# First layer's modulation vectors 2 to 5: dot products on VectorE in place of products on TensorE

## The chip, the cores and the metric

The kernel runs on one core of a Trainium2 chip. The metric is the device time of one launch in microseconds. Before the change it is 2318.97 us, the median of three runs (2317.82 to 2321.76).

## The reference

Two layers of a trunk over 640 tokens of width 1024: 128 context tokens and 512 latent tokens that share all weights. Each layer first computes its modulation from the conditioning vector (one for each of the two token groups), six vectors of 1024:

```
mod_ctx = silu(c_ctx) @ w_mod[l] + b_mod[l]      # w_mod[l]: 1024 x 6144
mod_lat = silu(c)     @ w_mod[l] + b_mod[l]
sh1, sc1, g1, sh2, sc2, g2 = split(mod, 6)       # vectors 0 to 5
h = rmsnorm(x, norm1_g) * (1 + sc1) + sh1
x = x + g1 * mixer(h)                            # attention, conv, pool, gMLP; gates; w_out
h = rmsnorm(x, norm2_g) * (1 + sc2) + sh2
x = x + g2 * (relu(h @ w_mlp_in) ** 2 @ w_mlp_out)
```

Vectors 0 and 1 are needed at the very start of a layer, vector 2 where the mixer's output projection is added, 3 and 4 at the second norm, 5 in the MLP. All is float32, and the large matrix products are made of three products of split operands (high by high, high by low, low by high).

## The kernel before

**Tiling.** Activations lie with 128 channels on the partitions and the 640 tokens along the free axis. Weights come as slabs of 128x1024 (512 KB). Each slab is loaded by SP into one of four buffers tagged `raw` (L251, L235), and split by ACT (`h`, L240) and VectorE (`l`, L241) into one of three pairs of buffers. TensorE multiplies from these at L362, in output tiles of 128x640 with 48 or 24 matmuls.

**Order of the work.** TensorE and SP run in the order in which the program is written out (`manual_schedule`). On VectorE, ACT and GpSimd a list scheduler decides: among instructions that are ready it takes the one that was written out first, and `later(-n)` moves an instruction n places ahead (slab splits by 2500, evacuations of PSUM by 1000). From gates(3) to the second gate of branch 1 VectorE too runs in written order (`byhand`, L1251 to L1284). A layer of the mixer goes: q, k, v and rotary (`qk`); attention, into which `_weave` (L1241) mixes the products of `fill()` (two convolution inputs, L948, and eight gates of branch 0, L1120); the gMLP's v (`sgu_v`, L1016); branch 0 and the gMLP outputs; gates and branches 3, 2; gates of branch 1 with the end of the convolution (`conv_out`); branch 1; the output projection (`project`, L554).

**Attention's chain.** For each head and each of four blocks of queries: scores in PSUM (L846), row maximum on VectorE (L848), exponential on ACT (L849), reciprocal and scaling on VectorE (L850, L851). For each of five blocks of keys (L857): transposes into the one PSUM buffer `pt`, a copy to `h` by ACT (L240), a subtraction to `l` by VectorE (L241), then two products with the values (L865). The buffer `pt` is free for the next key block when the subtraction is done.

**Modulation.** Vectors 0 and 1 of layer 0 come from `start()` (L1170) on TensorE. Vectors 2 to 5 of layer 0 come from `mod_steps` (L429): blocks of `w_mod` are loaded into two `md` buffers (L439), multiplied on TensorE by silu(c) as 32-column weights in four column groups (L447), copied by ACT (L450), transposed (L454), copied again (L456) and added up on VectorE (L460, L461). All of layer 1's vectors come from `mod_dots` (L464) during layer 0's MLP: rows of the transposed `w_mod` are loaded into `raw` buffers (one block is 128 outputs by 1024 inputs), and VectorE multiplies each with silu(c), once for each token group, and accumulates along the row (L490).

**Side work.** Both are generators in the list `side`; `tick()` (L500) runs the first one up to its next `yield`, and `flush()` runs all to the end. `mod_steps` is appended before gates(3) and is advanced by the ticks of gates and branches from there to the `flush()` before branch 1 (L1287).

Of the kernel before, what the change touches and what calls it, by code (L numbers as in the profile page):

```python
# [140 lines left out]
def trunk(ctx, tc, a, o):  # L141
# [287 lines left out]
    def mod_steps(l, g, mk):  # L429

        wv = a["w_mod"].rearrange("d (v h n) -> d v h n", v=6, h=2)
        bm = lcol[l][:, C_BMOD:C_BMOD + 48].rearrange("p (v c) -> p v c", v=6)
        for half in range(2):
            for kp in range(4):
                rr = []
                for i in range(2):
                    k = 2 * kp + i
                    t_ = mk().rearrange("p (v n) -> p v n", v=2)
                    sp.dma_start(out=t_, in_=wv[k * P:(k + 1) * P, 2 * g:2 * g + 2, half, :])  # L439
                    rr.append([t_[:, j] for j in range(2)])  # L440
                    yield
                if kp == 0:
                    t = psum("pt")
                for i in range(2):
                    for j in range(2):
                        q = 2 * i + j
                        pe.matmul(t[32 * q:32 * q + 32], sv3[:, 2 * kp + i, :], rr[i][j], start=kp == 0, stop=kp == 3)  # L447
            rows, cols = tmp(512), tmp(512)
            with later(-EVAC_FIRST):
                act.activation(rows, t, AF.Copy)  # L450
            yield
            tr = psum("pt")
            for nb in range(4):
                pe.transpose(tr[:, nb * P:(nb + 1) * P], rows[:, nb * P:(nb + 1) * P], ident)  # L454
            with later(-EVAC_FIRST):
                act.activation(cols, tr, AF.Copy)  # L456
            tv = cols.rearrange("p (n q m) -> p q n m", q=4, m=32)
            for j in range(2):
                dst = mod3(l, 2 * g + j)[:, 4 * half:4 * half + 4, :]
                vec.tensor_tensor(dst, tv[:, j, :, 0:2], tv[:, 2 + j, :, 0:2], ALU.add)  # L460
                vec.tensor_tensor(dst, dst, bm[:, 2 * g + j, 4 * half:4 * half + 4, None].to_broadcast([P, 4, 2]), ALU.add)  # L461
            yield True

    def mod_dots(l, mp):  # L464


        sw, junk = maker(mp, "sw", 1, 2 * D)(), maker(mp, "junk", 1, D)
        sp.dma_start(out=sw, in_=a["crow"])
        th_ = junk()
        s3 = [sw[:, s * D:(s + 1) * D] for s in range(2)]  # L470
        yield
        for z in s3:
            act.activation(th_, z, AF.Tanh, scale=0.5)
            vec.scalar_tensor_tensor(z, th_, 1.0, z, ALU.add, ALU.mult)
        bm = lcol[l][:, C_BMOD:C_BMOD + 48].rearrange("p (v c) -> p v c", v=6)
        blocks = [(v, c) for v in (1, 0, 2, 4, 3, 5) for c in range(KC)]

        def fetch(v, c):
            t = raw_tile()
            sp.dma_start(out=t, in_=a["w_modt"][v, c])  # L480
            return t

        w = fetch(*blocks[0])
        yield
        for i, (v, c) in enumerate(blocks):
            wn = fetch(*blocks[i + 1]) if i + 1 < len(blocks) else None
            dst = mod3(l, v)
            for s in range(2):
                out = w if s else junk()
                vec.scalar_tensor_tensor(out, w, 0.5, s3[s], ALU.mult, ALU.mult, accum_out=dst[:, c, s:s + 1])  # L490
            if c == KC - 1:
                vec.tensor_tensor(dst, dst, bm[:, v, :, None].to_broadcast([P, KC, 2]), ALU.add)
            w = wn
            yield
# [3 lines left out]
    taps = [iter(())]  # L498

    def tick(n=0):  # L500
        for _ in range(n):
            next(taps[0], None)
        while side:
# [631 lines left out]
    def branch(bi, gs, br, merged, mg):  # L1135
        for mp in range(4):
            w = use("b", bi, mp)
            for m in (2 * mp, 2 * mp + 1):
# [8 lines left out]
                tick(TAPS[1])  # L1147
# [61 lines left out]
    for l in range(DEPTH):  # L1209
# [3 lines left out]
        with opened(f"mx{l}") as mx:  # L1213
# [13 lines left out]
            with opened(f"at{l}") as ap:  # L1227
# [4 lines left out]

                def fill():
                    for c in range(2, 4):
                        ys.append((yield from conv_in(l, c, h, cv)))
# [251 lines left out]
```

## Time and profile before

| | |
|---|---|
| median of three runs | 2318.97 us |
| the profiled execution's own time | 2326.15 us |
| its span, first to last instruction | 2324.4 us |
| mean granted TensorE clock | 0.992 |
| TensorE busy | 2254.2 us (97%) |
| VectorE busy | 1655.0 us (71%) |
| ACT busy | 856.4 us (37%) |
| GpSimd busy | 70.4 us (3%) |
| stages, by the trace | attention of layer 0 about 118 to 272 us, gates(3) from 364, `flush()` before branch 1 at about 647, output projection from 676, layer 1 from 1192 |

A matmul's busy time overlaps the next one's, so pitches (from one start to the next) are used for TensorE. Idle time of an engine is the length of a stretch less its busy time there.

### The profile page before, as it was taken

To read this page: it belongs to the slowest core of one execution; us is meant where nothing else is said; L and a number is where in the kernel's file an instruction comes from. 1 tells how busy PE (TensorE), PEld (TensorE's weight loads), DVE (VectorE), ACT (ScalarE), POOL (GpSimd) and SP (SyncE) were. 2 spreads that over 40 slices of the span, in tenths; PEclk is the share of its full clock that TensorE was granted. 3 is DMA by queue.
4 is the path that set the end of the run, shared out by engine and by line. 5 is a ranking of instruction groups with operands and counts; after the bars stand their busy time and mean duration, and the time that the engine had idled before them with its cause. 6 is when DMAs were issued, how large, how long until landed. Compare 5 with 4: busy or idle time off the path is not lost.

```text
span 2324.4 us, 36290 instructions
## 1 busy us (share of the span) xinstructions
PE 2254.2 (97%) x15050; PEld 2182.7 (94%) x15050; DVE 1655.0 (71%) x2557; ACT 856.4 (37%) x1296; POOL 70.4 (3%) x188
## 2 busy tenths in 40 slices
PE   6999999999999999999999999999999999999997
PEld 5989899989999999999998898999999999999987
DVE  6676457678777776766477773687897788777776
ACT  5455342222335332222254553422224453232233
POOL 1100000000000000000011000000000000000001
PEclk9999999999999999999999999999999999999999
DMA  7421122333343444444354212222222432222223
GB/s 285 113 84 60 63 70 99 133 136 136 126 138 127 154 154 146 151 148 146 108 175 107 78 46 69 73 78 64 65 76 92 150 109 65 73 85 89 73 91 110
DMA packets 77253, 252.43 MB, mean 109 GB/s; under 512 B 11808, under 2 KB 12832, under 8 KB 76960
## 3 DMA queue, kind: packets, MB, share of 16 engines
q1 hardware_dynamic: 66592, 224.56, 29.9%
q0 software_dynamic: 9920, 24.89, 3.8%
q8 instruction: 118, 1.93, 0.3%
q10 hardware_dynamic: 576, 0.66, 0.1%
q14 instruction: 47, 0.39, 0.1%
HBM read 238.65 MB, written 10.75 MB: 107 GB/s over the span
## 4 chain that ended last, share of the span: by engine, by line
PE 66%; issue 24%; DVE 6%; ACT 2%; DMA 1%; POOL 0%; SPq 0%; DVEq 0%; ACTq 0%; POOLq 0%
PE ps L362 44%; PE ph L362 5%; PE pt L653 4%; DVE l L241 2%; PE sc L653 2%; PE pt L857 1%; PE sc L846 1%; PE po L865 1%; PE sc L362 1%; ACT h L240 1%; PE po L653 1%; PE sc L1031 1%; DMA st<-in_w_mod 1%; PE pt L447 1%; PE sc L414 1%
## 5 line engine op out<-in xcount | busy, mean ns | idle before, releaser
L362 PE MATMUL ps<-h,h 128*128 128x320 f32 x5296 | 1119.3, 310 | 12.8 <-ACT gx L1132 4.7
L362 PEld LDWEIGHTS ps<-h,h 128*128 128x128 f32 x5296 | 862.7, 188 | 31.9 <-ACT h L240 12.5
L362 PE MATMUL ps<-h,l 128*128 128x320 f32 x3408 | 835.7, 309 | 0.0
L240 ACT ACTIVATE h<-raw 128x1024 fp32r<-128x1024 f32 x337 | 357.2, 1060 | 976.7 <-PE ps L362 658.8
L362 PEld LDWEIGHTS ps<-h,l 128*128 128x128 f32 x3408 | 585.6, 188 | 0.0
L241 DVE TENSOR_TENSOR l<-raw,h 128x1024 fp32r<-128x1024 f32 x337 | 411.6, 1222 | 217.5 <-ACT h L240 217.1
L362 PE MATMUL ps<-l,h 128*128 128x320 f32 x1520 | 384.6, 308 | 0.0
L362 PEld LDWEIGHTS ps<-l,h 128*128 128x128 f32 x1520 | 263.9, 188 | 0.3
L973 DVE SCALAR_TENSOR_TENSOR cv<-cv,cw,cv 128x655 f32<-128x655 f32 x240 | 215.9, 899 | 6.1
L554 DVE SCALAR_TENSOR_TENSOR x<-ps,mod,x 128x128 f32<-128x128 f32 (+2 forms) x260 | 99.8, 434 | 117.9 <-PE ps L362 117.8
L362 PE MATMUL ph<-h,h 128*128 128x320 f32 x768 | 179.6, 318 | 0.0
L362 PEld LDWEIGHTS ph<-h,h 128*128 128x128 f32 x768 | 129.1, 188 | 7.2
L240 ACT ACTIVATE h<-tmp 128x640 fp32r<-128x640 f32 (+1 forms) x92 | 67.5, 737 | 138.7 <-DVE tmp L1311 79.9
L362 PE MATMUL ph<-h,l 128*128 128x320 f32 x384 | 118.5, 309 | 0.0
L362 PE MATMUL ps<-bo,h 128*128 128x320 f32 x512 | 96.5, 309 | 1.8 <-DVE mg L1144 1.8
L241 DVE TENSOR_TENSOR l<-pt,h 128x512 fp32r<-128x512 f32 x84 | 57.9, 689 | 41.5 <-ACT h L240 41.3
L362 PEld LDWEIGHTS ps<-bo,h 128*128 128x128 f32 x512 | 80.2, 188 | 5.1 <-DVE mg L1144 2.4
L241 DVE TENSOR_TENSOR l<-tmp,h 128x640 fp32r<-128x640 f32 x92 | 74.9, 816 | 8.3 <-ACT h L240 8.3
L240 ACT ACTIVATE h<-pt 128x512 fp32r<-128x512 f32 x84 | 50.3, 599 | 77.1 <-PE pt L857 70.8
L490 DVE SCALAR_TENSOR_TENSOR junk<-raw,sw 128x1024 f32<-128x1024 f32 x48 | 58.8, 1224 | 25.4 <-DMA raw<-in_w_modt 25.2
L653 PE MATMUL pt<-h,h 128*128 128x320 f32 x260 | 71.4, 309 | 2.6 <-DVE tmp L659 2.6
L362 PEld LDWEIGHTS ph<-h,l 128*128 128x128 f32 x384 | 72.1, 188 | 0.0
(300 smaller groups left out, 2573.9 us busy)
## 6 DMA issues: line engine op xcount, KB each, us to landing
raw<-in_slabs SPq DMA_DIRECT2D x324, 512.0 KB, 3.6
raw<-in_w_modt SPq DMA_DIRECT2D x48, 512.0 KB, 3.7
md<-in_w_mod SPq DMA_DIRECT2D x32, 512.0 KB, 4.4
q<-qd POOLq DMA_DIRECT2D x18, 256.0 KB, 3.1
st<-in_w_mod SPq DMA_DIRECT2D x8, 512.0 KB, 9.7
raw<-in_w_mod SPq DMA_DIRECT2D x8, 512.0 KB, 7.1
x<-in_x SPq DMA_DIRECT2D x8, 320.0 KB, 6.0
qd<-h POOLq DMA_DIRECT2D x8, 320.0 KB, 9.1
```

Of the source, the lines that this page charges most:

```text
L240: act.activation(h, src, AF.Copy)
L241: (eng or vec).tensor_tensor(lo, src, _f(h), ALU.subtract)
L362: pe.matmul(v[:, c0:c1] if half is None else v, w_[:, kk, :], x_[:, c0:c1], start=first and pi == 0, stop=last and pi == 2)
L414: pe.matmul(v[:, c0:c1], ones, src[:, c0:c1], start=True, stop=True)
L447: pe.matmul(t[32 * q:32 * q + 32], sv3[:, 2 * kp + i, :], rr[i][j], start=kp == 0, stop=kp == 3)
L490: vec.scalar_tensor_tensor(out, w, 0.5, s3[s], ALU.mult, ALU.mult, accum_out=dst[:, c, s:s + 1])
L554: vec.scalar_tensor_tensor(xc[:, c0:c1], v[:, c0 - b0:c1 - b0], gv[:, c, s:s + 1], xc[:, c0:c1], ALU.mult, ALU.add)
L653: pe.matmul(v, w_[:, k0 + k, :], x_, start=k == 0 and pi == 0, stop=k == 3 and pi == 2)
L846: pe.matmul(v[:, c0:c1], lq, kk[:, SEQ + c0:SEQ + c1], start=pi == 0, stop=pi == 1)
L857: pe.transpose(pt[:, qt * P:(qt + 1) * P], parts[hd, qt][:, j * P:(j + 1) * P], ident)
L865: pe.matmul(po, vt[:, 1 + j, hd // 4, :], halves[hd, j][pi], start=j == 0 and pi == 0, stop=j == 4 and pi == 1)
L973: vec.scalar_tensor_tensor(y, b[:, j:j + CO], cw[:, c * CONV_K + j:c * CONV_K + j + 1], y, ALU.mult, ALU.add)
```

## The change

`mod_steps` goes. `mod_dots` takes the list of vectors, the source and, optionally, a `junk` maker. In layer 0 it computes vectors 2, 4, 3, 5 (32 blocks of 512 KB from `w_modt0`, the transposed rows). There it has no 1024-wide junk buffer: the first token group's dot of a block is made in two halves of 512 with outputs in `tmp` buffers and added up by a small `tensor_tensor`; the second group's writes over the block itself. silu(c) is made from `crow` (1 MB, both token groups, repeated on all partitions) in four pieces of 512.

The generator's first step issues the load of `crow`, the second makes silu and loads block 0, each later one loads block i+1 and computes block i. The ticks: two after each of the two convolution inputs and each of the eight gates in `fill()` (20, so blocks 0 to 17); one for every second tile of branch 0 (4, blocks 18 to 21); none while `hold` is set, from gates(3) to the second gate of branch 1; one for each of the last six gates of branch 1 (blocks 22 to 27); the other four in `flush()`. The `md` pool (2 x 4 KB a partition) goes, `sw` (8 KB) moves into the mixer's pool for all of layer 0's mixer, and `dynamic_dma_scratch_size` falls from 4096 to 2048.

```diff
-    def mod_steps(l, g, mk):
...
-    def mod_dots(l, mp):
+    def mod_dots(l, mp, vs, src, junk=None):
-        sw, junk = maker(mp, "sw", 1, 2 * D)(), maker(mp, "junk", 1, D)
+        sw = maker(mp, "sw", 1, 2 * D)()
         sp.dma_start(out=sw, in_=a["crow"])
-        th_ = junk()
         s3 = [sw[:, s * D:(s + 1) * D] for s in range(2)]
         yield
-        for z in s3:
+        for c0 in range(0, 2 * D, 512):
+            z, th_ = sw[:, c0:c0 + 512], tmp(512)
             act.activation(th_, z, AF.Tanh, scale=0.5)
             vec.scalar_tensor_tensor(z, th_, 1.0, z, ALU.add, ALU.mult)
...
+        def dot(out, w, z, acc):
+            vec.scalar_tensor_tensor(out, w, 0.5, z, ALU.mult, ALU.mult, accum_out=acc)
...
-            for s in range(2):
-                out = w if s else junk()
-                vec.scalar_tensor_tensor(out, w, 0.5, s3[s], ALU.mult, ALU.mult, accum_out=dst[:, c, s:s + 1])
+            if junk:
+                dot(junk(), w, s3[0], dst[:, c, 0:1])
+            else:
+                acc = small(2)
+                for hf in range(2):
+                    cs = slice(512 * hf, 512 * hf + 512)
+                    dot(tmp(512), w[:, cs], s3[0][:, cs], acc[:, hf:hf + 1])
+                vec.tensor_tensor(dst[:, c, 0:1], acc[:, 0:1], acc[:, 1:2], ALU.add)
+            dot(w, w, s3[1], dst[:, c, 1:2])
...
-        while side:
+        while side and not hold[0]:
...
-                tick(TAPS[1])
+                if bi or m % 2:
+                    tick(TAPS[1])
...
+                if l == 0:
+                    side.append(mod_dots(0, mx, (2, 4, 3, 5), "w_modt0"))
                 def fill():
                     for c in range(2, 4):
                         ys.append((yield from conv_in(l, c, h, cv)))
+                        for _ in range(2):
+                            tick()
                     for m in range(KC):
                         yield from gate(0, m, h, gs, True)
+                        for _ in range(2):
+                            tick()
...
-                mdp = ExitStack()
-                md = maker(mdp.enter_context(opened(f"md{l}")), "md", 2, 1024)
-                if l == 0:
-                    side.extend([mod_steps(l, 1, md), mod_steps(l, 2, md)])
+                hold[0] = True
...
                         _run(gate(1, m, h, gs))
+                        hold[0] = m < 2
                         tick(LATE_TAPS if m < 2 else 0)
...
-                mdp.close()
...
-                side.append(mod_dots(l + 1, mp))
+                side.append(mod_dots(l + 1, mp, (1, 0, 2, 4, 3, 5), "w_modt", maker(mp, "junk", 1, D)))
...
-    nc = _bacc.Bacc("TRN2", target_bir_lowering=False, num_devices=1, dynamic_dma_scratch_size=4096)
+    nc = _bacc.Bacc("TRN2", target_bir_lowering=False, num_devices=1, dynamic_dma_scratch_size=2048)
```

## Rows read from the trace of the kernel before

**Rows 1.** The page: busy time of the engines; the span in 40 slices with the busy tenths of TensorE and VectorE and the granted clock.
```profile
PE 2254.2 (97%) x15050; PEld 2182.7 (94%) x15050; DVE 1655.0 (71%) x2557; ACT 856.4 (37%) x1296; POOL 70.4 (3%) x188
...
PE   6999999999999999999999999999999999999997
...
DVE  6676457678777776766477773687897788777776
...
PEclk9999999999999999999999999999999999999999
```

**Rows 2.** TensorE's waits (engine, tile and line that waited, whom for: us in total, times, longest), both layers together: that of the transposes L857; then, of that line alone with its weight loads counted in, who was waited for (us, times).
```profile
PE pt L857 <- DVE sm L850: 4.8, 4, 1.2
...
  DVE l L241: 6.8, 14
```

**Rows 3.** The removed products: TensorE in order of time about one of the 16 groups of L447 and one of the four of L454 (start us, us, what).
```profile
385.51 1.07 PE L447 MATMUL pt<-md,silu 128*32 128x512 f32 x8
386.50 0.70 PE L362 MATMUL ps<-h,h 128*128 128x320 f32 x3
...
439.49 0.60 PE L454 MATMUL pt<-ident,tmp 128*128 128x128 f32 x4
439.84 0.68 PE L362 MATMUL ps<-h,h 128*128 128x320 f32 x3
```

**Rows 4.** The chain that ended last (start us, us, what), at the first and the last tile of the stretch in which layer 0 has the products; then the same two tiles of layer 1, which has none.
```profile
364.41 21.17 PE ps L362 x144
...
618.12 7.04 PE ps L362 x48
...
1521.12 84.25 PE ps L362 x574
...
1757.14 7.05 PE ps L362 x48
```

**Rows 5.** VectorE in order of time in layer 0's MLP, about one block of the dots of layer 1.
```profile
803.69 1.23 DVE L490 SCALAR_TENSOR_TENSOR junk<-raw,sw 128x1024 f32<-128x1024 f32 x1 [0.82 <-DMA raw<-in_w_modt]
804.84 0.08 DVE L490 DVE_READ_ACCUMULATOR junk<-raw,sw 128x1 f32 x1
804.84 0.82 DVE L241 TENSOR_TENSOR l<-tmp,h 128x640 fp32r<-128x640 f32 x1
```

**Rows 6.** VectorE's groups in attention of layer 0, 118 to 264 us.
```profile
L241 DVE TENSOR_TENSOR l<-pt,h 128x512 fp32r<-128x512 f32 x42 | 28.9, 689 | 20.7 <-ACT h L240 20.6
...
L850 DVE RECIPROCAL sm<-sm 128x1 f32<-128x1 f32 x32 | 5.1, 160 | 5.2 <-ACT p L849 4.4
```

**Rows 7.** Stretches of layer 0's mixer: length, then busy time (and count) of PE, PEld, DVE, ACT, POOL, then clock, DMA share, GB/s.
```profile
118.00:264.00 146.00, 138.54 (x922) 130.77 (x921) 101.04 (x178) 79.34 (x166) 4.32 (x8) 1.00 0.20 62
...
264.00:300.00 36.00, 36.00 (x177) 30.57 (x176) 8.22 (x11) 7.91 (x12) 1.37 (x3) 1.00 0.31 96
300.00:336.00 36.00, 35.09 (x239) 34.78 (x238) 25.23 (x37) 18.19 (x32) 0.00 (x0) 1.00 0.22 74
...
596.00:626.00 30.00, 30.00 (x202) 28.36 (x200) 18.64 (x27) 10.25 (x14) 0.00 (x0) 1.00 0.44 153
626.00:648.00 22.00, 22.00 (x151) 21.91 (x151) 17.58 (x26) 14.34 (x18) 0.00 (x0) 1.00 0.23 73
648.00:684.00 36.00, 35.02 (x237) 34.53 (x236) 24.80 (x30) 11.09 (x15) 4.33 (x8) 1.00 0.46 147
```

**Rows 8.** The gates' evacuations in attention (L1128; layer 0 has 16 of the 32): duration ns, first and last start.
```profile
L1128 ACT ACTIVATE gx<-ph,bgh x32: 508/527/547, 179.3 to 1429.8; 128x320 f32<-128x320 f32 x32
```

**Rows 9.** Inside one head, about one key block: TensorE, ACT, VectorE, TensorE; then VectorE about the next key block.
```profile
206.76 0.60 PE L857 MATMUL pt<-ident,p 128*128 128x128 f32 x4
...
207.46 0.60 ACT L240 ACTIVATE h<-pt 128x512 fp32r<-128x512 f32 x1 [1.98 <-PE pt L857]
...
208.09 0.69 DVE L241 TENSOR_TENSOR l<-pt,h 128x512 fp32r<-128x512 f32 x1 [0.74 <-ACT h L240]
...
208.98 0.60 PE L857 MATMUL pt<-ident,p 128*128 128x128 f32 x4
...
210.31 0.69 DVE L241 TENSOR_TENSOR l<-pt,h 128x512 fp32r<-128x512 f32 x1 [0.69 <-ACT h L240]
```

**Rows 10.** DMAs: issues by line with KB each and median us to landing; then SP's slab loads in attention (start of the first, us to the end of the last, count).
```profile
raw<-in_slabs SPq DMA_DIRECT2D x324, 512.0 KB, 3.6
raw<-in_w_modt SPq DMA_DIRECT2D x48, 512.0 KB, 3.7
...
gx<-in_rope POOLq DMA_DIRECT2D x4, 320.0 KB, 4.7
sw<-in_crow SPq DMA_DIRECT2D x1, 1024.0 KB, 6.8
...
161.42 52.07 SPq L251 DMA_DIRECT2D raw<-in_slabs  x5
```

**Rows 11.** The end of `qk` in layer 0, in the columns of rows 7: the stretch before attention in which the clock falls.
```profile
94.00:98.00 4.00, 2.47 (x12) 1.67 (x11) 3.26 (x5) 2.35 (x3) 2.14 (x4) 0.96 0.52 72
98.00:101.00 3.00, 2.31 (x7) 1.40 (x6) 0.82 (x1) 0.72 (x2) 0.00 (x0) 0.50 0.88 133
101.00:104.50 3.50, 3.50 (x10) 2.61 (x11) 0.22 (x1) 1.96 (x2) 0.00 (x0) 0.50 0.66 163
```

More of the change, by code (lines that the diff above doesn't have):

```diff
@@ L427, in mod3 @@
         return modc[l].rearrange("p (v c s) -> p v c s", v=6, s=2)[:, v]
-    def mod_steps(l, g, mk):
[L431 to L462, printed above, removed]
-    def mod_dots(l, mp):
-        sw, junk = maker(mp, "sw", 1, 2 * D)(), maker(mp, "junk", 1, D)
+    def mod_dots(l, mp, vs, src, junk=None):
+        sw = maker(mp, "sw", 1, 2 * D)()
         sp.dma_start(out=sw, in_=a["crow"])
-        th_ = junk()
         s3 = [sw[:, s * D:(s + 1) * D] for s in range(2)]
         yield
-        for z in s3:
+        for c0 in range(0, 2 * D, 512):
+            z, th_ = sw[:, c0:c0 + 512], tmp(512)
             act.activation(th_, z, AF.Tanh, scale=0.5)
@@ L475, in mod_dots, with fetch @@
         bm = lcol[l][:, C_BMOD:C_BMOD + 48].rearrange("p (v c) -> p v c", v=6)
-        blocks = [(v, c) for v in (1, 0, 2, 4, 3, 5) for c in range(KC)]
-        def fetch(v, c):
+        blocks = [(n, c) for n in range(len(vs)) for c in range(KC)]
+        def fetch(n, c):
             t = raw_tile()
-            sp.dma_start(out=t, in_=a["w_modt"][v, c])
+            sp.dma_start(out=t, in_=a[src][n, c])
             return t
+        def dot(out, w, z, acc):
+            vec.scalar_tensor_tensor(out, w, 0.5, z, ALU.mult, ALU.mult, accum_out=acc)
         w = fetch(*blocks[0])
         yield
-        for i, (v, c) in enumerate(blocks):
+        for i, (n, c) in enumerate(blocks):
             wn = fetch(*blocks[i + 1]) if i + 1 < len(blocks) else None
-            dst = mod3(l, v)
-            for s in range(2):
-                out = w if s else junk()
-                vec.scalar_tensor_tensor(out, w, 0.5, s3[s], ALU.mult, ALU.mult, accum_out=dst[:, c, s:s + 1])
+            dst = mod3(l, vs[n])
+            if junk:
[7 more added lines that the diff above has]
+            dot(w, w, s3[1], dst[:, c, 1:2])
             if c == KC - 1:
-                vec.tensor_tensor(dst, dst, bm[:, v, :, None].to_broadcast([P, KC, 2]), ALU.add)
+                vec.tensor_tensor(dst, dst, bm[:, vs[n], :, None].to_broadcast([P, KC, 2]), ALU.add)
             w = wn
@@ L496, in trunk @@
     side = []
-    taps = [iter(())]
+    taps, hold = [iter(())], [False]
     def tick(n=0):
@@ L1449, in _arrays @@
     r["cvec"] = np.stack([_col(i["c"][0]), _col(i["c_ctx"])], axis=2).reshape(P, -1)
-    r["w_mod"] = i["w_mod"][0]
     w0 = i["w_mod"][0][:, :2 * D].reshape(4, 2, P, 2, 4, 256)
     r["w_mod0"] = w0.transpose(4, 0, 2, 1, 3, 5).reshape(4, 4, P, 1024)
-    r["w_modt"] = i["w_mod"][1].T.reshape(6, KC, P, D)
+    r["w_modt0"] = i["w_mod"][0].T.reshape(6, KC, P, D)[[2, 4, 3, 5]]
+    r["w_modt"] = i["w_mod"][1].T.reshape(6, KC, P, D)[[1, 0, 2, 4, 3, 5]]
     r["crow"] = np.repeat(np.concatenate([i["c"][0], i["c_ctx"]])[None], P, axis=0)
```

## The prediction

> **What bounds the kernel now.** I read the page's engine line and slices first. TensorE is busy 2254.2 us of the span, at nine tenths or more in 38 of 40 slices and at the full clock, while VectorE has 71% [rows 1]. So what is taken out of TensorE's stream shortens the time by its full pitch, and what makes TensorE wait lengthens it. The table of waits comes next: within the stages the waits are small, and among the steady ones are those of attention's transposes L857 for VectorE [rows 2]. Then the stretches [rows 7]: in attention, 118 to 264 us, TensorE is idle for 146 - 138.5 = 7.5 us; where its removed products stand it hardly idles at all. The change thus takes work from the engine that sets the time and gives it to one that TensorE waits for in the very stage where most of it lands. The two sums follow.
>
> **What goes from TensorE.** The eight records of one group of L447 start at 385.51, and the next slab's matmul starts at 386.50: 0.99 us [rows 3]. (The 605 ns of one record is latency and would give five times that.) There are 16 such groups: 15.8 us. Four transposes L454 hold TensorE from 439.49 to 439.84, 0.35 us, four times: 1.4 us. Together 17.2 us. A second way needs no pitch: layer 1 runs the same stretch without these products. Between the same two tiles the chain takes 618.12 - 364.41 = 253.71 us in layer 0 and 1757.14 - 1521.12 = 236.02 us in layer 1 [rows 4], so 17.7 us, small waits included. I take 17.7, all of it on the path. The ACT copies and the small VectorE additions of `mod_steps` go as well; they lay beside TensorE's work, so I give them nothing.
>
> **What comes to VectorE.** A dot over 1024 starts at 803.69, and the next instruction, with the accumulator read beside it, at 804.84: 1.15 us [rows 5]. No dot over 512 is in the trace. Half of 1.15, 0.58 us, is below it; above it is the 0.69 us of a 128x512 subtraction [rows 6] with 0.08 us for a read that isn't covered [rows 5], 0.77. By the subtraction less the same overlap (1.23 - 1.15) I take 0.61. The small addition is nearest to the reciprocal of one column, 0.16 us [rows 6]; with overlap 0.12. One block is 2 x 0.61 + 0.12 + 1.15 = 2.5 us (2.4 to 2.9), and 32 of them 80 us; silu(c) is four pieces of 0.61, 2.4 us. The question is what lies there already.
>
> **Attention, 18 blocks.** The gates' evacuations run from 179.3 to 273.1, eight gates [rows 8], some 13 us each, so six gates are behind by 264, where the last head ends. With the second convolution input before them, 2 + 12 = 14 blocks are written out ahead of work of that last head. They need 14 x 2.5 + 2.4 = 37.4 us, and VectorE is idle for 146 - 101.0 = 45.0 us [rows 7]. It fits, but VectorE is then 95% full. SP runs ahead as far as buffers allow, so blocks land early and dots are ready before their place in the program. The scheduler takes older work first; so a dot that is ahead of its place yields to the softmax chain and only fills gaps. It can't be broken off, though, and VectorE's gaps before subtractions are 0.74 and 0.69 us [rows 9]. A dot begun in one overshoots: when something becomes ready during a dot, the mean rest is the sum of squares over twice the sum, (2 x 0.61^2 + 1.15^2) / (2 x 2.37) = 0.44 us. Where does that reach TensorE? The subtraction that starts at 208.09 ends at 208.78, and the transposes into the one `pt` buffer start at 208.98 [rows 9]: slack 0.2 us. By the order of the units three places of a head are as tight (transposes 1 and 4, last value product); the others have a unit more between. With 8 heads, 24 places. Dots fill 37.4 / 45.0 = 83% of the gaps, so the delay is 0.83 x 0.44 = 0.37 us, less part of the slack 0.3: 24 x 0.3 = 7 us. The ends: 0 if all goes into gaps that nothing waits behind; and if the dots run at their ticks in pairs, 5 us at a time, less the idle of such a time (5 x 45.0/146 = 1.5), 7 pairs cost 24 us. I take 7.
>
> **The other 14 blocks.** From 264 to 300 (the gMLP's v) VectorE is idle for 27.8 us, room for blocks 14 to 17; from 300 to 336 it is idle for 10.8 us [rows 7] for blocks 18 to 21, 10 us. The gMLP's chain is older and goes first. I take 0.5 us, ends 0 and 3. Blocks 22 to 31: VectorE is idle for 11.4 us in 596 to 626, 4.4 us to 648 and 11.2 us to 684 [rows 7], 27 us for 25 us of dots. The four of `flush()` are written out before branch 1's additions and the splits of `merged`, so they go ahead of them, and the output projection waits for the last split already (TensorE loses 1.0 us in that stretch). I take 1.5 us; ends 0 and 6, since 7 blocks left over at 648 would be 17.5 us against 11.2.
>
> **DMAs and queues.** The block loads are as many and as large as before, 32 of 512 KB, on SP; `crow` adds 1 MB, 6.8 us to landing, with no reader near. They now share the slabs' four `raw` buffers, and in SP's order a block that waits for a buffer holds the slab behind it. Slabs are loaded in attention about every 13 us (five in 52.07 us) and land in 3.6 us [rows 10]; with a block or two between slabs at least one gate's time of lead is left. So I give nothing; were the cover gone, each of the 12 slabs of `fill()` could show its 3.6 us. GpSimd's queue gets no new DMA. Its scratch is halved: the trace doesn't show how many transfers it held, so from 0 to one more landing, 4.7 us [rows 10], at the start of each layer; I take 0. Addresses shift by the pools' sizes, which may add or spare a wait of a `reuse_waits` pool: 1 us either way.
>
> **Sum.** -17.7 + 7 + 0.5 + 1.5 = -8.7 us. The profiled execution's own time is 2326.15, 7.2 us over the median of the runs; the terms are stretches of it and hold for both: 2326.15 - 8.7 = 2317.5 there, and 2318.97 - 8.7 = 2310.3 us for the median.
>
> **Rivals.**
> (a) *All hidden.* The 45.0 us of idle time take the dots and TensorE waits for none. For it: layer 0's MLP already holds 96 such dots beside a TensorE that doesn't idle. Against: there a tile is 7 us long and nothing waits within a microsecond, as in rows 9. 2318.97 - 17.5 = 2301.5 us.
> (b) *VectorE becomes the bound in attention.* One mechanism: dots that are past their place in the program are older than the softmax work behind them and go first, so each pair stops the chain. Price 24 us as above, with 1.5 + 0.5 later: 2318.97 - 17.7 + 26 = 2327.3 us, slower. For it: 95% full, gaps shorter than a dot. Against: the blocks land ahead. It decides from the point where TensorE's idle time in 118 to 264 grows by over 15.7 us (17.7 less the 2 later), from 7.5 to 23.
> (c) *A draw.* The same stalls at 13 to 18 us: 2318 us.
> (d) *The clock.* Before attention TensorE is busy for only 2.47 us of 94 to 98, and after that its granted clock is 0.50 (1.2 GHz) from 98 to 104.5 [rows 11]: 6.5 us at half speed lose 3.25 us. In attention the clock is 1.00 with 7.5 us of idle time in small pieces [rows 7]. If the stalls bunched so that it fell three times, 10 us on top of the forecast: 2320 us, a draw. The Trainium skill (TensorE: Matmul & The Clock Gate, HAM oscillation — how this bites in real kernels) warns of just this: pauses between bursts of matmuls let the clock drop, and each next burst starts at the low rate. By it 94 to 104.5 is such a case; no row shows attention in it.
> (e) *Not what it says.* The scheduler may put many attention dots behind 264. Then the gain is nearer to (a); it is in that chance.
>
> **How the numbers follow.** Forecast 0.42 (2305 to 2314.3), (a) with (e) 0.20, (b) 0.20, (c) 0.13, (d) 0.05. A difference under 0.2%, 4.6 us, can't be told from none. Faster by more: 0.42 + 0.20 = 0.62. Within it: 0.13 + 0.05 = 0.18. Slower by more: 0.20. The range takes all of (a), with 1 us for shifted waits, from 2300.5, and reaches into (b) to 2326, leaving about half of that and a little below out; the likeliest case's own is 2305 to 2314.3.
>
> **What would show it.** TensorE's stretch of rows 4 should be 236 us in layer 0, as in layer 1. Attention from 118 to its last transposes should be some 7 us longer, with L857's waits for `l` grown most and VectorE above nine tenths; if instead VectorE idles while TensorE waits, it stands before a block's DMA, and my ordering is wrong. The scheduler is the weak point: if pairs of blocks stand unbroken before subtractions, (b) holds. Slab waits of L240 in attention would say that the shared buffers were too few; a longer load of rope or `place` at a layer's start would speak against the smaller scratch; a wait of more than 3 us before the output projection against my 1.5.

## The result, and the profile after

The changed kernel takes 2348.9 us (median of four runs, 2348.0 to 2353.0) against 2318.9 us for the kernel before in the same session: ratio 1.0131 [1.0113, 1.0149], 30 us slower. The profiled execution took 2352.99 us, its span 2351.1. The prediction was 2310.3 us, range 2300.5 to 2326.

The page of the changed kernel, as in [rows 1]: busy time, then TensorE, VectorE and the granted clock in 40 slices.

```profile
PE 2246.8 (96%) x14906; PEld 2186.8 (93%) x14906; DVE 1728.0 (73%) x2775; ACT 855.2 (36%) x1294; POOL 70.7 (3%) x188
...
PE   6998899999899999999999999999999999999998
...
DVE  6778767688887776767476765577897788777776
...
PEclk9999999999999999999999999999999999999999
```

VectorE's share grew by two points only. Besides the first and the last, TensorE's slices 4, 5 and 11 are below nine tenths now; a slice is 58.8 us, so that is 176 to 294 us, most of it attention, and 588 to 647, the last stage of the mixer. Where the time went is read by finding the same matmul in both traces and subtracting its starts; this difference is called the lag below, and its growth over a stage is what the stage loses. Before attention the changed profile is 3.2 us ahead (the clock fall of [rows 11] is missing in it, as in the trace of the kernel before with the smaller scratch, below). Then attention loses 23.5 us, the gMLP outputs 5.2, the stretch that held the products gains 15.1, the end of the mixer loses 18.2; the rest of the program adds next to nothing (-1.1).

Attention first, as in [rows 7]: one row of the kernel before and two of the changed one. The first of the two goes from the matmul at 118.00 before to that at 258.00 before, so both stretches hold the same 895 matmuls; the second is the worst piece of it.

```profile
118.00:258.00 140.00, 133.93 (x895) 126.68 (x893) 98.67 (x175) 76.94 (x162) 4.09 (x7) 1.00 0.21 64
```

```profile
114.83:278.30 163.47, 143.16 (x895) 133.44 (x893) 132.29 (x279) 79.75 (x166) 5.66 (x9) 0.95 0.33 102
...
226.00:250.50 24.50, 19.70 (x130) 18.09 (x129) 22.87 (x52) 11.37 (x24) 0.00 (x0) 0.99 0.34 111
```

140.00 us became 163.47. VectorE does 33.6 us more, yet it is idle for 31 us of the longer stretch: over the whole stage it is not full. In the second row it is nearly full and TensorE idles for 4.8 of 24.5 us. The work comes in lumps, and the timeline of VectorE (start us, us, what) shows one:

```profile
183.32 0.68 DVE L847 TENSOR_TENSOR tmp<-po,tmp 64x512 f32<-64x512 f32 x1 [1.59 <-ACT tmp L843]
183.93 0.67 DVE L449 SCALAR_TENSOR_TENSOR tmp<-raw,sw 128x512 f32<-128x512 f32 x1
...
184.53 0.68 DVE L449 SCALAR_TENSOR_TENSOR tmp<-raw,sw 128x512 f32<-128x512 f32 x1
...
185.15 0.68 DVE L449 SCALAR_TENSOR_TENSOR tmp<-raw,sw 128x512 f32<-128x512 f32 x1
...
185.76 0.68 DVE L449 SCALAR_TENSOR_TENSOR tmp<-raw,sw 128x512 f32<-128x512 f32 x1
...
186.37 0.81 DVE L822 TENSOR_REDUCE sm<-sc 128x1 f32<-128x640 f32 x1
...
187.18 1.21 DVE L449 SCALAR_TENSOR_TENSOR raw<-raw,sw 128x1024 f32<-128x1024 f32 x1
...
188.32 0.68 DVE L241 TENSOR_TENSOR l<-pt,h 128x512 fp32r<-128x512 f32 x1
```

Two blocks' half dots stand unbroken for 2.4 us, then whole dots stand one by one between the instructions of softmax. Block 2, the first of the two, had been asked for at 162.6 and landed at 166.2, long before 183.9. The dots did not run when they could, but as pairs where the two ticks of a gate stand in the program; here, as in four of attention's nine groups of half dots, right behind one of attention's sums over `tmp` buffers (L847). The transposes (L831, formerly L857) wait for the subtraction L241 behind such a lump. TensorE's waits in the whole program, first that of the kernel before, then as in [rows 2]:

```profile
PE pt L857 <- DVE l L241: 1.8, 4, 0.7
```

```profile
PE pt L831 <- DVE l L241: 15.7, 11, 2.5
...
PE sc L414 <- DVE c L957: 8.0, 1, 8.0
...
PE pt L831 <- DVE sm L824: 5.1, 3, 2.7
```

The second line of the changed kernel is the last stage: L414 is the convolution's column sum, and it waits for the sum of the four convolved channels (L957). The same two instructions of TensorE, before and after:

```profile
616.12 0.46 PE L362 MATMUL ps<-h,l 128*128 128x320 f32 x2
...
616.85 1.27 PE L414 MATMUL sc<-c,ones_c 128*128 128x328 f32 x4
```

```profile
626.50 0.46 PE L362 MATMUL ps<-h,l 128*128 128x320 f32 x2
635.00 2.55 PE L414 MATMUL sc<-c,ones_c 128*128 128x328 f32 x4 [8.04 <-DVE c L957]
```

The lag of 10.4 us (626.50 - 616.12) becomes 18.2 (635.00 - 616.85) and 20.3 right behind it; 7.8 more are lost where branch 1 starts, behind the last splits of the convolution's output. The chain of work that ended last, 600 to 640 us of the changed kernel, tells why:

```profile
605.52 3.53 DMA raw<-in_w_modt
609.07 1.31 DVE tmp L449 x4
610.38 0.81 DVE cv L947
611.27 1.15 DVE raw L449 x2
...
615.33 3.65 DMA raw<-in_w_modt
619.00 1.31 DVE tmp L449 x4
...
622.36 3.49 DMA raw<-in_w_modt
```

A block's load starts when a split slab gives its buffer free (L241), VectorE runs the block's dots when it has landed, does a convolution tap or two (L947) and slab splits, and comes to the next block. It stands idle before four blocks for 3.3 us in all. The taps behind the dots were written out earlier, and wait all the same.

### The profile page after: what moved, and what is told of

Its sections match the earlier page's. It is cut to its first block, busy times and chain, and to the rows that moved or that the text cites. A ratio compares the mean times of both kernels' runs of the same rounds, so it can differ in the third digit from the quotient of the medians.

```text
span 2351.1 us, 36212 instructions
## 1 busy us (share of the span) xinstructions
PE 2246.8 (96%) x14906; PEld 2186.8 (93%) x14906; DVE 1728.0 (73%) x2775; ACT 855.2 (36%) x1294; POOL 70.7 (3%) x188
## 4 chain that ended last, share of the span: by engine, by line
PE 79%; DVE 13%; ACT 3%; issue 2%; DMA 2%; POOL 0%; DVEq 0%; SPq 0%; ACTq 0%
PE ps L362 59%; PE ph L362 4%; PE pt L627 4%; DVE l L241 3%; PE sc L627 2%; PE sc L362 2%; ACT h L240 1%; DVE tmp L449 1%; PE pt L831 1%; PE po L839 1%; DVE cv L947 1%; PE po L627 1%; PE sc L820 1%; PE sc L1005 1%; DVE raw L449 1%
## 5 line engine op out<-in xcount | busy, mean ns | idle before, releaser
L241 DVE TENSOR_TENSOR l<-raw,h 128x1024 fp32r<-128x1024 f32 x337 | 411.5, 1221 | 173.0 <-ACT h L240 173.0
L947 DVE SCALAR_TENSOR_TENSOR cv<-cv,cw,cv 128x655 f32<-128x655 f32 x240 | 215.9, 899 | 5.9
L449 DVE SCALAR_TENSOR_TENSOR junk<-raw,sw 128x1024 f32<-128x1024 f32 x48 | 58.8, 1224 | 54.3 <-DMA raw<-in_w_modt 54.2
L449 DVE SCALAR_TENSOR_TENSOR raw<-raw,sw 128x1024 f32<-128x1024 f32 x80 | 97.5, 1219 | 0.3
L241 DVE TENSOR_TENSOR l<-pt,h 128x512 fp32r<-128x512 f32 x84 | 57.7, 687 | 36.5 <-ACT h L240 36.3
L241 DVE TENSOR_TENSOR l<-tmp,h 128x640 fp32r<-128x640 f32 x92 | 75.0, 817 | 9.2 <-ACT h L240 9.1
```

The source lines that it names most:

```text
L241: (eng or vec).tensor_tensor(lo, src, _f(h), ALU.subtract)
L449: vec.scalar_tensor_tensor(out, w, 0.5, z, ALU.mult, ALU.mult, accum_out=acc)
L947: vec.scalar_tensor_tensor(y, b[:, j:j + CO], cw[:, c * CONV_K + j:c * CONV_K + j + 1], y, ALU.mult, ALU.add)
```

## Experiments

Fifteen kernels ran, each with the kernel before on the same chip. Each result is the median time, then its ratio to the kernel before with a 95% interval. "Loss in attention" is the lag gained over the 895 matmuls above, from one profile of each kernel; two kernels that leave attention as it was (the scratch alone, and the first version for use) give 0.0 and -0.1 us. Line numbers in the rows are each kernel's own, and `...` marks where an edit is shown in part.

**The scratch alone.**

```diff
-dynamic_dma_scratch_size=4096
+dynamic_dma_scratch_size=2048
```

> The kernel before with the scratch of 2048 alone. Theory A (the loss is VectorE's time for the dots, standing in the way of softmax, taps and splits): the scratch is innocent, 2315 to 2323 us. Rival S (a smaller scratch, so descriptors or addresses, slows GpSimd's loads and with them the stages): a part of the 30 us is here, 2325 us or more.

The result is 2319.7 us, 0.9994 [0.9983, 1.0005]: the scratch costs nothing that can be told from none. Its trace also serves as a second one of the kernel before.

**Dots of 8 columns, everything else kept; then only those of attention.**

```diff
+            if l == 0:
+                out, w, z = out[:, :8], w[:, :8], z[:, :8]
...
+            if l == 0 and at_[0] < 18:
+                out, w, z = out[:, :8], w[:, :8], z[:, :8]
```

> The changed kernel, every fetch, buffer, tick and instruction kept, but each of layer 0's dots goes over 8 columns in place of 512 or 1024 (it leaves out most of the products of vectors 2 to 5). Theory A (VectorE's time): what is left is TensorE's gain of 17.7 and the small fixed price of the dots, 2298 to 2308 us. Rival R (the blocks in the slabs' four buffers and on SP hold the slabs back): the loss stays, 2335 us or more. Rival S: 2325 or more.

> The changed kernel with the dots of blocks 0 to 17 alone cut to 8 columns, so those of attention (it leaves out most of the products of vector 2, 4 and the first two blocks of 3); blocks 18 to 31 are whole. Theory A with the offsets read from the two traces: attention's 23.5 us go, gMLP's 5.2 and the last stage's 18.2 stay: 2325 us (2321 to 2330). Rival C (the clock: TensorE's falls behind the bursts make the loss, and come back wherever work bunches): most of the loss stays, 2335 or more. Rival R: 2340 or more.

The first takes 2312.2 us, 0.9957 [0.9942, 0.9972], a little above theory A's 2298 to 2308 and far from the rivals'. The stretch from the matmul at 364.4 to that at 620 of the kernel before is 17.7 us shorter, the term of the forecast to a tenth. Two losses stay without the dots' length: 4.4 us in attention where silu is made (2.9 in one wait of the transposes, 1.5 right behind it), and 4.3 us at the convolution's norm, where VectorE stands before blocks that are not there yet (us in total, times, longest):

```profile
DVE tmp L451 <- DMA raw<-in_w_modt: 5.8, 4, 2.5
```

The second takes 2330.9 us, 1.0041 [1.0026, 1.0055], just above theory A's range of 2321 to 2330: attention loses 4.4 instead of 23.5 us, the last stage still 17.4. Its attention, the same 895 matmuls:

```profile
114.97:259.41 144.44, 135.69 (x895) 128.02 (x893) 105.40 (x279) 79.31 (x166) 6.45 (x11) 0.99 0.37 117
```

So most of both losses goes with the dots' own time on VectorE. The loads alone, with every buffer and SP's order kept, leave no more than the 4.4 and 4.3 us.

**A buffer of their own for what the first group's dots write.**

```diff
+        jk = None if junk else maker(mp, "jk", 1, 256)().bitcast(mybir.dt.bfloat16)
...
-                    dot(tmp(512), w[:, cs], s3[0][:, cs], acc[:, hf:hf + 1])
+                    dot(jk, w[:, cs], s3[0][:, cs], acc[:, hf:hf + 1])
```

> The changed kernel, whole, but the first token group's half dots write to a buffer of their own (512 columns in two bytes each) and no longer to the six tmp buffers that attention's sums also use. Theory G (a dot that needs a tmp buffer must wait for attention's own users of that buffer ahead of it and holds up those behind it, so dots can't run early in gaps and stand in pairs at their ticks): attention's loss falls from 23.5 to 0 to 10 us, 2325 to 2337 us, and the bursts of four half dots in a row are gone. Rival V (it is the volume alone, VectorE too full whatever the order): 2344 to 2350.

The result is 2346.8 us, 1.0107 [1.0085, 1.0129], the rival's figure: attention still loses 23.4 us. Yet the bursts of four half dots are gone, as theory G said, and 19 blocks, not 14, run there. So the shared `tmp` buffers made the bursts, but the bursts alone did not make the loss. VectorE now also stands before loads:

```profile
PE pt L831 <- DVE l L241: 16.9, 14, 2.7
...
DVE jk L449 <- DMA raw<-in_w_modt: 7.1, 10, 1.4
```

**The same dots without loads,** over silu(c) itself, in halves and with their own buffer.

```diff
...
+            if l == 0:
+                return sw[:, 0:D]
             t = raw_tile()
...
```

> The changed kernel with all 32 blocks' dots at their ticks, as many columns and as long, but over silu(c) itself in place of the loaded blocks, four half dots a block with a buffer of their own for what they write: no block is fetched, no raw buffer held, no tmp buffer shared (it computes wrong values for vectors 2 to 5). Theory F (the forecast's picture is right once nothing holds the dots: a ready dot only fills gaps, and the loss in attention came from late data and shared buffers): attention loses 3 to 11 us, silu included, the last stage nothing, 2305 to 2313 us. Rival V (VectorE goes through its instructions in an order fixed when the kernel was built, and a dot placed there before a softmax instruction holds that one up however early its data are): attention loses 20 us or more, 2321 to 2341 us.

The result is 2317.3 us, 0.9987 [0.9978, 0.9997], between the two. Attention loses 13.9 us although it now holds 19.5 blocks, and VectorE is 95% busy:

```profile
113.91:267.84 153.93, 137.65 (x895) 127.55 (x893) 145.83 (x377) 79.98 (x166) 6.30 (x11) 0.99 0.21 62
```

There is more work on VectorE and less loss, so volume is not the cause. But this kernel differs from the last in two things, no loads and no whole dots. (It says nothing on the last stage: with no load to wait for, all 32 blocks stand ahead of gates(3), 21 of them up to the matmul at 264.)

**Those two apart.** All dots in halves; then a lead of two blocks for the loads; then both. All three have the own buffer.

```diff
...
-            dot(w, w, s3[1], dst[:, c, 1:2])
...
+                acc = small(2)
+                for hf in range(2):
+                    cs = slice(512 * hf, 512 * hf + 512)
+                    dot(jk, w[:, cs], s3[1][:, cs], acc[:, hf:hf + 1])
+                vec.tensor_tensor(dst[:, c, 1:2], acc[:, 0:1], acc[:, 1:2], ALU.add)
```

```diff
...
-        w = fetch(*blocks[0])
+        lead = 1 if junk else 2
+        ws = [fetch(*b) for b in blocks[:lead]]
...
```

> The kernel with the dots' own buffer (e4_junk) and every 1024-wide dot cut into two of 512, so that no piece of a dot is longer than 0.6 us. The run without loads lost 14 us in attention with 21 blocks in halves, the one with the own buffer 23.4 with 19 blocks in halves and wholes. Theory W (the whole dots, 1.15 us in one piece, overshoot): attention loses 14 us or less, 9 less in all, 2335 to 2339 us. Rival D (VectorE stands in its fixed order before a block that is still on its way, 7.1 us in ten waits, and late blocks push dots to bad places): attention still loses 20 or more, 2344 to 2349.

> The kernel with the dots' own buffer (e4_junk), each block fetched two ahead of its dots in place of one; dots in halves and wholes as there. Theory D (late blocks): the waits of VectorE for blocks in attention fall from 7.1 us to under 2, attention loses 14 to 17 us, and the last stage's waits shrink too, 2334 to 2341 us. Theory W (size of a piece): unchanged, 2344 to 2349. Rival R (the four shared raw buffers): blocks held longer make slabs late, above 2349.

> Both edits, fetched two ahead and all dots in halves, in their own buffer: what the run without loads had, but with the loads. If late blocks and long pieces are all that stood between attention's 23.4 us there and the 14 us without loads, attention loses 14 us here, with 7 to 15 left in the last stage: 2328 to 2338 us. If neither matters (the order of VectorE is what it is), 2344 or more.

With halves the time is 2330.0 us, 1.0045 [1.0031, 1.0059], below theory W's 2335 to 2339, and attention loses 12.0 us. With a lead of two it is 2345.3 us, 1.0116 [1.0095, 1.0137], and 23.7 us. With both it is 2334.4 us, 1.0069 [1.0052, 1.0086], and 15.6 us. The halves' attention:

```profile
114.31:266.28 151.97, 137.21 (x895) 127.68 (x893) 142.15 (x362) 80.17 (x166) 6.31 (x11) 0.99 0.40 121
```

So whole dots hurt and the lead doesn't help. But the lead lowered VectorE's waits for blocks in attention only from 7.1 to 5.4 us, while the halves lowered them to 1.9, so theory D was not put to the test (first the lead's waits, then the halves'):

```profile
DVE jk L449 <- DMA raw<-in_w_modt: 5.4, 8, 1.3
```

```profile
DVE jk L449 <- DMA raw<-in_w_modt: 1.9, 3, 1.1
```

**Length or writing over the block.** The second group's halves write over the block again; then also without the own buffer, the first group's in `tmp`.

```diff
...
-                    dot(jk, w[:, cs], s3[1][:, cs], acc[:, hf:hf + 1])
+                    dot(w[:, cs], w[:, cs], s3[1][:, cs], acc[:, hf:hf + 1])
```

> The kernel with all dots in halves (e8_halves) with one thing put back: the second token group's halves write over the block itself again, as the whole dots did. Theory W (the length of a piece): attention loses 12 us as there, 2328 to 2333 us. Rival P (what hurt in the whole dot was that it writes over the block and so must come last): attention loses 20 or more, 2340 or more.

> The changed kernel with the second group's dots in halves over the block itself and no buffer of their own: the first group's halves write to tmp as in the change. Theory W alone: 12 us in attention, 2328 to 2333 us. Theory G as a second condition (halves help only where a dot can leave its place, and the tmp buffers hold it there): the bursts stay and attention loses 17 to 24, 2336 to 2347 us.

The first takes 2348.9 us, 1.0120 [1.0099, 1.0141], the number of rival P; the second 2356.3 us, 1.0159 [1.0136, 1.0182], worse than either theory. Halves that write over the block lose 24.4 and 27.0 us in attention. The order of VectorE's instructions differs from the halves' above: in the first of the two, a half of one token group and a half of the other stand together in 20 places, so that a piece is 1.2 us long again:

```profile
169.23 0.68 DVE L449 SCALAR_TENSOR_TENSOR jk<-raw,sw 128x512 bf16<-128x512 f32 x1
...
169.84 0.69 DVE L449 SCALAR_TENSOR_TENSOR raw<-raw,sw 128x512 f32<-128x512 f32 x1
```

The table counts such stretches in the traces over the 895 matmuls (a stretch is what stands between two other instructions of VectorE: dots, their reads and their small additions; a 0.1 us reciprocal of 128x4 is not counted as a break):

```
kernel                        loss us   blocks   stretches over 1 us   longest us
changed kernel                  23.5     14.0            18                3.7
vector 5 in the MLP             23.2     14.0            18                3.7
own buffer                      23.4     19.0            21                2.7
own buffer, lead of two         23.7     20.0            23                2.7
halves over the block           24.4     19.0            25                2.7
halves over the block, tmp      27.0     14.0            20                3.8
halves, lead of two             15.6     19.2             7                3.0
halves, no loads                13.9     19.5             7                2.2
halves                          12.0     18.0            10                2.1
quarters                         5.9     13.4            10                1.7
last version (below)             4.0     12.9             7                2.2
```

There are two clusters, and the count of long stretches parts them where blocks, buffers and lead do not. Any threshold from 0.8 to 1.1 us leaves the same clusters. Within the lower one the count doesn't order the losses (7 stretches go with 4.0 and with 15.6 us). (The second of the three versions below is not in the table: it has 9 such stretches, and one of them, 7.8 us with a wait in it, makes most of its loss.)

One rival parts the kernels with their own buffer in much the same way: VectorE's waits for blocks in attention are 7.1, 5.4 and 7.3 us in those of the upper cluster and at most 2.3 in those of the lower. The changed kernel and the one with halves over the block in `tmp` have no such wait there and lose 23.5 and 27.0, so it isn't what costs them. What part of the 12.4 us between the two runs with halves, 12.0 and 24.4, it makes, no run separates. The row of the halves over the block is this:

```profile
DVE jk L449 <- DMA raw<-in_w_modt: 7.3, 10, 1.1
```

**Quarters.** Eight pieces of 256 a block.

```diff
...
+                for q in range(8):
+                    cs = slice(256 * (q // 2), 256 * (q // 2) + 256)
+                    dot(jk, w[:, cs], s3[q % 2][:, cs], acc[:, q:q + 1])
```

> The kernel with its own buffer and each dot cut into four pieces of 256 (eight pieces a block, 0.3 us each, more VectorE time in all by the eight short reads). Theory W carried on (the overshoot goes with the length of a piece): attention's 12 us, of which 4 to 5 are silu, fall to 7 to 9, 2324 to 2329 us. Rival V2 (by now it is VectorE's volume and its fixed price per piece): 12 us or more, 2330 to 2336.

The result is 2327.2 us, 1.0036 [1.0023, 1.0049], as theory W has it. In attention:

```profile
118.10:263.96 145.86, 134.13 (x895) 126.62 (x893) 136.10 (x421) 78.98 (x166) 4.78 (x8) 1.00 0.34 108
```

VectorE is busy for 136.10 us here and for 132.29 in the changed kernel, and the stretch is 17.6 us shorter. Of the 5.9 us lost, 2.9 are the wait at silu; the granted clock stays at 1.00. The last stage still loses 11.3 us.

**The last stage: vector 5 in the MLP.**

```diff
...
-                    side.append(mod_dots(0, mx, (2, 4, 3, 5), "w_modt0"))
+                    side.append(mod_dots([(0, v, "w_modt0", n) for n, v in enumerate((2, 4, 3))], mx))
...
+                side.append(mod_dots([(0, 5, "w_modt0", 3)] + [(1, v, "w_modt", n) for n, v in enumerate((1, 0, 2, 4, 3, 5))],
+                                     mp, maker(mp, "junk", 1, D)))
...
```

> The changed kernel with vector 5's eight blocks moved to the front of the dots in layer 0's MLP (first needed there), so that two blocks in place of ten are left for the stage before the output projection. Theory A (the late loss of 18.2 us is the blocks' dots and their waits for data among taps, convolution norm and splits): 14 to 18 us of it go and the MLP takes the eight for nothing, 2331 to 2335 us. Rival L (the stage is late because VectorE brings its backlog from attention and branch 0 along): 2343 or more.

The result is 2334.3 us, 1.0064 [1.0050, 1.0078]: theory A's figure. From 614 to 655 of the kernel before the lag goes from 8.6 to 8.2 us, where the changed kernel's goes from 10.4 to 28.6. With two blocks in place of ten the stage loses nothing, though it is entered with nearly the same lag.

**Versions for use.** The first takes half of the change: vector 2's dots in the gMLP's v stage, 5's in the MLP, 3 and 4 on TensorE as before.

```diff
...
+                    v2 = mod_dots([(0, 2, "w_modt0", 0)], mx)
...
+                if (5 * s + b) % 2 == 0:
+                    next(other, None)
...
+                    side.append(mod_steps(l, 3, md))
...
```

> A version for use: vector 2's dots and silu go into the gMLP's v stage, where VectorE is idle for 27.8 of 36 us, vector 5's into layer 0's MLP, and vectors 3 and 4 stay on TensorE as one run of the old products; no dot in attention, none before the output projection. Theory A: half of the 17.7 us is gained and nothing paid, 2310 us (2308 to 2313). Rival: silu and eight blocks don't hide in the gMLP stage, or a half of the old products costs more than half of their time, 2316 or more.

The second edit is in `sgu_v`. The result is 2309.1 us, 0.9958 [0.9945, 0.9970], as forecast. Its gMLP v stage, to be read against the second of [rows 7]:

```profile
260.00:296.00 36.00, 36.00 (x178) 30.77 (x177) 31.02 (x73) 9.95 (x16) 1.59 (x3) 1.00 0.63 200
```

VectorE's 8.2 us became 31.0, and TensorE is busy for all 36: the dots are hidden entirely. The second version has no old products at all: `crow`, silu and block 0 are asked for ahead of attention, and every block is in quarters.

```diff
...
+                    dots = mod_dots([(0, 4, "w_modt0", 1), (0, 3, "w_modt0", 2), (0, 2, "w_modt0", 0)], mx)
+                    next(dots)
+                    next(dots)
...
+                        if l == 0:
+                            next(dots)
...
+                        for _ in range(2 if l == 0 and m < 7 else 0):
+                            next(dots)
...
```

> A version for use without any of the old products: every block in eight pieces of 256 with a buffer of its own, silu made at the end of the stage before attention, vectors 4 and 3 in attention (16 blocks), vector 2 in the gMLP's v stage, vector 5 in layer 0's MLP; none before the output projection. Theory W (what counts in attention is how long VectorE is held in one piece): 17.7 us gained, 1 to 3 paid for the dots in attention, 0 to 3 for silu and the gMLP stage, 2302 to 2307 us, below e7_split's 2309. Rival V2 (about 0.4 us a block whatever the pieces): 7 us paid in attention and 3 elsewhere, 2309 to 2314.

The result is 2317.3 us, 0.9990 [0.9980, 0.9999], neither theory's. From 134 to 258 of the kernel before the dots cost 3.5 us, close to theory W, but 12.5 us were lost between 118 and 134. Shown are ACT and VectorE in order of time, TensorE's wait, and two stretches.

```profile
122.92 0.37 ACT L872 ACTIVATE tmp<-sc,sm 128x128 f32<-128x128 f32 x1
...
123.58 0.17 DVE L873 RECIPROCAL sm<-sm 128x4 f32<-128x4 f32 x1
...
130.69 0.42 DVE L448 SCALAR_TENSOR_TENSOR jk<-raw,sw 128x256 f32<-128x256 f32 x1 [6.83 <-DMA raw<-in_w_modt]
...
131.04 0.68 DVE L875 TENSOR_TENSOR tmp<-tmp,sm 128x512 f32<-128x512 f32 x1
```

```profile
PE pt L879 <- DVE mod L464: 8.6, 1, 8.6
```

```profile
118.00:138.00 20.00, 9.97 (x57) 9.38 (x56) 11.51 (x41) 6.25 (x18) 1.85 (x3) 0.74 0.49 140
...
125.70:135.80 10.10, 3.93 (x16) 3.96 (x17) 4.36 (x15) 0.60 (x1) 0.57 (x1) 0.50 0.38 130
```

One dot stood before block 1, which was still on its way, and all of attention's start stood behind it; the granted clock fell to half on top (0.50 from 125.7 to 135.8, 0.74 in the mean). This is the plainest sight of the mechanism: the softmax scaling L875 needs the reciprocal L873 of 123.58 and the exponentials L872, the last of which starts at 122.92, and it runs at 131.04, right behind the late dot. VectorE did not pass over the instruction whose data were late, though another was ready.

```diff
...
-                        if l == 0:
-                            next(dots)
...
-                        for _ in range(2 if l == 0 and m < 7 else 0):
+                        for _ in range(2 if l == 0 else 0):
```

> e15_fine without the two ticks after the convolution inputs: block 1 is asked for and multiplied from the first gate on, and the 16 blocks stand at two a gate. There VectorE stood 6.83 us before block 1, which was still on its way, with the softmax chain behind it in the fixed order, and 12.5 us were lost in 118 to 134; from 134 to 258 the 16 blocks cost 3.5 us. Theory O (the order is fixed: one dot put before data that are late is what cost 12.5): those go and nothing else changes, 2303 to 2308 us. Rival B (VectorE's backlog from silu and the first block ahead of attention): 2313 to 2318 as before.

The two ticks after the convolution inputs are gone, and the last gate has two in their place. The result is 2309.6 us, 0.9949 [0.9935, 0.9963] (the kernel before read 2321.4 beside it), 1.6 us above theory O's range and well below rival B's 2313. Attention loses 4.0 us, 1.7 of them in 118 to 134, where 12.5 were lost. But not all else is as it was: from 300 to 336, the gMLP outputs, 3.9 us are lost where the version before lost 0.6. Why was not followed up. The first and the last version beat both kernels by their intervals; between them the runs do not decide.

## Why the prediction was wrong, point by point

**What bounds the kernel, and what goes from TensorE: right.** 17.7 us was forecast from [rows 4] and 17.7 measured with short dots. In the changed kernel itself 15.1 show up to the matmul at 626.50, 2.1 less than with short dots up to there. The 2.1 are lost inside the stretch, where TensorE waits 3.2 us for VectorE's products with the gates (1.3 with short dots); no run shows why.

```profile
PE ps L362 <- DVE gx L1118: 3.2, 4, 1.6
```

(Rival (a) takes off 17.5 where the term is 17.7; the 0.2 us decide nothing.)

**The duration of the pieces: right.** Four dots of 512 take 2.44 us from start to start (183.93 to 186.37), 0.61 each, and 0.61 was forecast.

**Attention: +23.5 us in place of +7.** The failed step is the sentence "a dot that is ahead of its place yields to the softmax chain and only fills gaps". It reads the scheduler as if it decided while the kernel runs. The scheduler fixes VectorE's order when the kernel is built, from modelled times (`schedule_with_timeline_sim`), and the chip follows it: the run in which VectorE stood for 6.83 us before a late block shows that it does not reorder. Nor were the dots ahead of their place. They write to the `tmp` buffers which attention's sums use too, so that they stood in pairs of blocks at their ticks, as rival (b) had it; with a buffer of their own the bursts were gone. The argument against (b), "the blocks land ahead", was true of the data and had no bearing. The count of 14 blocks ahead of the last head was right.

That (b)'s price of 24 us meets the 23.5 is in part luck. It reckons 7 pairs that stand unbroken for 5 us; in the trace the longest stretch is 3.7 us, and the 23.5 holds the 4.4 at silu and a share of the clock, which (b) does not have.

The prediction's arithmetic of overshoot was better than its use. Once a piece is 0.6 us or less and free to move, 18 blocks cost 12.0 us with silu, and 13.4 blocks in quarters 5.9. What was missing is that the cost turns on the unbroken piece: a stretch over 1 us, whether one whole dot or two halves together, is longer than the gaps of 0.69 to 0.74 us in [rows 9] and the slack of 0.2. That this comparison is the reason for the two clusters is argued, not shown. The sum of VectorE's idle time, 45.0 us, said nothing on that. And silu, 2.4 us of VectorE time thrown in with the dots, cost 4.4 with short dots around it.

**The gMLP outputs: +5.2 in place of 0.5 (ends 0 and 3).** The four blocks at branch 0's ticks delay the splits of the gated v; the same wrong step. Moving vector 2 into the stage ahead, where the idle time is real, cost nothing in the first version for use; in the last one the gMLP outputs lose 3.9.

**The last ten blocks: +18.2 in place of 1.5 (ends 0 and 6).** The idle time of 27 us was again summed, and who is in the way was asked only of branch 1's additions and the splits of `merged`. The convolution's last taps and its column sum were not in the list. The dots stand among them in VectorE's order, each block's behind a load that starts when a shared buffer comes free and lands some 3.5 us later. With short dots that waiting costs 4.3 us; the move of vector 5 took all 18.2 away.

**The clock.** Rival (d) was right as a companion: 0.95 in attention in place of 1.00. By an estimate from these rows it makes at most some 8 of the 23.5 us (0.05 of 163.47); its true share no run separates. The loss doesn't need it, since the run with halves over the block has 0.99 and loses 24.4 us:

```profile
115.78:280.19 164.41, 137.97 (x895) 127.60 (x893) 145.88 (x373) 80.01 (x166) 5.71 (x9) 0.99 0.36 113
```

**Queues and scratch: right** at nothing, with the one gap that a block's own lateness was left out where VectorE waits for it. Addresses were not tested by themselves.

It stays open why the scheduler sets halves of the two groups together when one writes over the block, and apart when both write elsewhere; only the orders were seen, not the reason. The clusters rest on one profile of each kernel.

## What to carry to other kernels

Do not take the sum of an engine's idle time for room for extra work: here the loss in attention fell from 23.5 to 5.9 us with a buffer of their own for the dots and pieces of 256 columns, though VectorE was busy for longer there (136.10 us against 132.29). Look at the gaps and the slack that the critical chain leaves there, and cut the work before placing it. VectorE's order was fixed before the run: what held an instruction back was its data, its buffers and whatever stood ahead of it, so a piece of side work needs a buffer that the chain doesn't use and data that are certain to be there. Side work is best put where the other engine depends on nothing from this one, as in the gMLP's v stage, where 22.8 us went in for nothing.

## What was not expected of the hardware

One late load of 512 KB made most of a loss of 12.5 us (1.7 without it), although VectorE stood for 6.83: TensorE waited 8.6 us, and its granted clock was at half rate from 125.7 to 135.8 us. The load itself took 13.3 us to land, where the median is 3.7; two transfers of GpSimd's queue that were issued beside it took 14.0 and 14.8:

```profile
raw<-in_w_modt SPq DMA_DIRECT2D x1, 512.0 KB, 13.3
qd<-h POOLq DMA_DIRECT2D x1, 320.0 KB, 14.0
qd<-l POOLq DMA_DIRECT2D x1, 320.0 KB, 14.8
```

Whether they slowed each other no run separates. The Trainium skill (PSUM — Partial Sum Buffer, Engine vs sequencer instructions) says that the queues of ScalarE, VectorE and GpSimd are strict first-in-first-out; this trace agrees for VectorE, with the 6.83 us.
